# Recurrent block's output product: two interleaved groups of four column tiles in place of one group and four single products

## The chip, the cores and the metric

The kernel runs on one core of one Trainium2 chip. The metric is the device time of one execution in microseconds (us); lower is better. The engines are named as in the profile: PE is TensorE (matmuls), PEld its weight loads, DVE is VectorE, ACT is ScalarE, POOL is GpSimd, and SP is SyncE, which only issues DMAs.

## The reference, cut to what matters

The kernel is a trunk of two layers over x (512 positions of 1024 channels, float32). Layer 0 mixes positions with an RG-LRU recurrent block, layer 1 with an S5 block, and each is followed by a ConvFFN. The change is in the last line of the recurrent block, a product of y (512 x 1024) with a 1024 x 1024 matrix, and the sum with h behind it.

```python
def _rglru_mixer(h, w_in, conv_w, conv_b, w_a, b_a, w_x, b_x, lam, w_out):
    xg = h @ w_in
    xr, gate = xg[..., :D_RNN], xg[..., D_RNN:]
    xr = _causal_dwconv(xr, conv_w, conv_b)
...
    _, hs = lax.associative_scan(_real_scan_combine, (a, bterm), axis=1)
    y = hs.astype(h.dtype) * jax.nn.gelu(gate)
    return y @ w_out

...
    for i in range(DEPTH):
        hn = _rmsnorm(h, norm_mix_g[i])
...
        h = h + mix.astype(h.dtype)
        hn = _rmsnorm(h, norm_ffn_g[i])
        h = h + _conv_ffn(hn, ffn_w_up[i], ffn_conv_w[i], ffn_conv_b[i], ffn_w_down[i]).astype(h.dtype)
```

## The kernel before

**Layout.** All activations lie transposed, channels on the 128 partitions and the 512 positions along the free axis, as 8 tiles of 128 x 512 per 1024 channels. The residual h is 8 such tiles in SBUF. So a product's column tile m is one PSUM bank of 128 x 512, summed over 8 contraction tiles k.

**Precision.** Each operand is split into a high part and a low part of a 32-bit type that TensorE takes at full rate. mm3 (L215 to 218) issues three matmuls for each pair of k and m: high by high (L216), low of the activation by high of the weight (L217), high by low of the weight (L218). Weights come from DRAM as raw; ScalarE casts whi<-raw (L212) and VectorE makes wlo<-raw,whi (L200). An activation's pair is called ah and al, or nh and nl, by the pool it lies in.

**Jobs.** The program is a list of jobs, run by run(). A weighted job has one 512 KB piece of a weight, and 24 matmuls of 128 x 512. There are 200 of them, numbered here from 0; weights are loaded and split some jobs ahead. Jobs without a weight run between two weighted ones. Work on a job's result is put off with defer(ticks, phase, fn, cost): it is issued so many jobs later, in one of four phases of that job. Of the time of VectorE in a job that isn't spent so (5.1 us less the costs), a credit is kept, and from it the items of a background list bg are issued. The engines' queues take their instructions in the order that a scheduler of the language makes of all this, by its own estimate of when each is ready.

**Two shapes of product.** group() runs four jobs, each with two contraction tiles k for four column tiles, so it fills four banks at once, k outermost. product() is one job for one column tile, all eight k in one bank. Banks come from two pools of four: psA (tiles called pa) and psB (pb, and py, pv, pr, px, stat, rb, sps).

**The output product.** project() (L471) is a group() over column tiles 0 to 3 in psA (here A0 to A3), then a product() for each of tiles 4 to 7 in psB. It is jobs 16 to 23, and the FFN's first group follows as jobs 24 to 27. Its operand is y: out(c) (L615) multiplies scan and gate for chunk c and makes its high and low part (al<-g,ah), chunks 4 and 5 one job before 6 and 7. The step with contraction tiles 2s and 2s+1 reads chunks 2s and 2s+1. residual() (L339) defers the sum h<-h,pb by 1 or 2 jobs, and in the same job the next norm's parts: nl<-h, and acc<-acc,sq. Behind tile 7's it defers the norm's stat (TensorE), v and r (VectorE) and rb.

**mid.** Between the group and the first single product, project() runs the unweighted job mid: it closes the recurrent block's buffers and calls then(), which opens the FFN's buffers and starts s5_pre. This fills bg with the preparation of S5's tables: matrices by channel block that go to DRAM (d_K, d_P, d_T), with small matmuls into sps and copies se<-sps. Its last item, finish, defers the transfers d_T<-d_K on GpSimd's queue.

**S5.** s5() comes after the FFN (from job 92). S_(c) makes pv of a transposed input us by a transfer from DRAM (d); H_(c) makes hs from the scan of v (VectorE, tables co and si); TR(c) makes py from us and hs by turns, and ys<-py goes through DRAM (d<-ys, ge<-d) to E_(c), which makes ah and al of it. J[c] are the last four products of S5's input, A0[.] and B0[.], with brackets, the steps of the GLU product that reads E_'s results.

Of the kernel before, what the change touches and what calls it, by code (L numbers as in the profile page):

```python
# [19 lines left out]
P = 128  # L20
S = 512
D = 1024
KD = D // P
# [48 lines left out]
class Trunk:  # L72
# [395 lines left out]
        else:  # L468
            yield from down(NPART - 1)

    def project(self, w, x, next_gain, view=lambda h, ps: (h, ps), turn=0, mid=None):  # L471

        def post(pss):
            self.turn = turn
            self.next_gain = next_gain
            for m in range(4):
                self.residual(m, pss[m], view, d=1 + m // 2)
        yield from self.group(w, x, self.bankA, post)
        if mid:
            yield Job(None, mid)  # L480
        for m in range(4, KD):
            yield self.product(w, m, x, self.bankB, lambda ps, m=m: self.residual(m, ps, view))


    def rglru(self, x, g_first, late_tables, gt, w_in, w_a, w_x, w_out, next_gain, then):
# [127 lines left out]
        yh, yl = [], []  # L613
# [54 lines left out]
            st["ctx"].close()  # L668
            then()

        yield from self.project(w_out, lambda: (yh, yl), next_gain, mid=mid)


    def small(self, pool, n, name, dt=F32):
# [775 lines left out]
def lay_out(inp):  # L1450

    import numpy as np

    def columns(*vs):
        return np.concatenate([np.reshape(v, (-1, P)) for v in vs]).T

    def blocks(w, rows):

        return w.reshape(-1, P, w.shape[1])[:rows].transpose(1, 0, 2).reshape(P, -1)

    def wide(w, c0, n):

        return [blocks(w[r:r + n * P, c0:c0 + 1024 // n], n) for r in range(0, w.shape[0], n * P)]

    def tiles(w):
        return np.stack(wide(w, 0, 2) + [blocks(w[:, c:c + P], KD) for c in range(4 * P, w.shape[1], P)])

    def mixed(w, axis):

        s = list(w.shape)  # L1470
        v = w.reshape(s[:axis] + [KD, NGC, GC] + s[axis + 1:])
        return v.swapaxes(axis + 1, axis + 2).reshape(s)

    def halves(re, im):

        r, i = (v.transpose(2, 0, 1).reshape(v.shape[2], -1) for v in (re, im))
        return np.stack([np.concatenate([r, i]), np.concatenate([i, r])], 1)

    g = {k: np.asarray(v) for k, v in inp.items()}
    a = np.stack([g["s5_a_re"][0].T, g["s5_a_im"][0].T], 1)  # L1480
    t = lambda v: v[0].swapaxes(1, 2)
    return dict(
        x=g["x"][0].T,
        cols=columns(g["norm_mix_g"], g["norm_ffn_g"], g["norm_final_g"], g["rg_conv_w"][0], g["rg_conv_b"],
                     g["rg_b_a"], g["rg_b_x"], g["rg_lambda"], g["s5_d"]),
        ffn_cols=np.stack([columns(g["ffn_conv_w"][i], g["ffn_conv_b"][i]) for i in range(2)]),
        rg_w_in=tiles(g["rg_w_in"][0]),
        rg_w_a=g["rg_w_a"][0].swapaxes(0, 1),
        rg_w_x=g["rg_w_x"][0].swapaxes(0, 1),
        rg_w_out=tiles(g["rg_w_out"][0]),  # L1490
        s5_w_in=tiles(mixed(g["s5_w_in"][0], 1)),
        s5_a=np.concatenate([a, a]),
        s5_log_dt=g["s5_log_dt"],
        s5_b=halves(t(g["s5_b_re"]), t(g["s5_b_im"])),
        s5_c=halves(g["s5_c_re"][0], g["s5_c_im"][0]),
        s5_w_glu=np.stack([v for c in range(0, 2 * D, 4 * P) for v in wide(mixed(g["s5_w_glu"][0], 0), c, 2)]),
        s5_w_out=tiles(g["s5_w_out"][0]),
        ffn_w_up=np.stack([tiles(w) for w in g["ffn_w_up"]]),
        ffn_w_down=np.stack([[v for q in range(NPART) for n in [2 if i and q == NPART - 1 else FP]
                              for c in range(0, D, 1024 // n) for v in wide(w[q * FP * P:(q + 1) * FP * P], c, n)]  # L1500
                             for i, w in enumerate(g["ffn_w_down"])]),
        fin=np.reshape(g["norm_final_g"], (1, D)),
    )
# [20 lines left out]
```

## Time and profile before

| | |
|---|---|
| three timed runs | 1194.86, 1195.45, 1198.6 us |
| their median | 1195.45 us |
| the profiled execution | 1200.28 us |
| its span, first to last instruction | 1198.5 us |
| granted TensorE clock over the span | 0.995 |
| busy share PE, DVE, ACT | 99%, 74%, 44% |

The profile tells what each engine did in one execution. Busy time counts running instructions. A row of the timeline has a start, the time from start to end (matmuls overlap, so two starts tell the rate and the row's time doesn't), and in brackets the idle time before it with the instruction whose end ended it. The granted clock is the share of TensorE's full speed (2.4 GHz; the lower level is half).

### The profile page before, as it was taken

What the parts mean: (1) busy time and instruction counts of PE and PEld (TensorE: products, weight loads), DVE (VectorE), ACT (ScalarE), POOL (GpSimd) and SP (SyncE); (2) the same over time, 40 slices, a digit from 0 to 9 for tenths busy, and PEclk for the clock granted to TensorE, in tenths of its full rate; (3) what the DMA queues carried; (4) which work ended last, traced back from release to release, by engine and by line L of the source; (5) the groups of instructions that cost most, each with busy time, mean ns of one, the idle gap of its engine ahead of it and who ended that gap; (6) DMA issues with size and microseconds to landing.
All of it is one profiled execution on the core that took longest, in us unless ns stands there. A gap on an engine that the chain in (4) does not pass through costs nothing.

```text
span 1198.5 us, 14366 instructions
## 1 busy us (share of the span) xinstructions
PE 1180.9 (99%) x5456; PEld 974.9 (81%) x5456; DVE 884.1 (74%) x1463; ACT 524.6 (44%) x701; POOL 18.6 (2%) x35
## 2 busy tenths in 40 slices
PE   9999999999999999999998999999999999999997
PEld 7777888888778888888898888888888888888886
DVE  7899799998998998678587442658766757575755
ACT  5588425434334242446267242524433434242425
POOL 0000000000000000202001000000000000000000
PEclk9999999999999999999999999999999999999999
DMA  7212422247554444546576523222232323233321
GB/s 272 71 70 88 140 93 89 93 125 257 203 163 124 145 143 149 181 162 229 158 223 222 157 89 106 88 98 96 90 104 89 105 91 103 90 103 92 102 88 71
DMA packets 77558, 154.65 MB, mean 129 GB/s; under 512 B 26481, under 2 KB 40193, under 8 KB 77361
## 3 DMA queue, kind: packets, MB, share of 16 engines
q1 hardware_dynamic: 73376, 138.79, 35.9%
q0 software_dynamic: 4112, 14.94, 3.5%
q8 instruction: 43, 0.70, 0.2%
q14 instruction: 27, 0.21, 0.1%
HBM read 132.21 MB, written 23.86 MB: 130 GB/s over the span
## 4 chain that ended last, share of the span: by engine, by line
PE 69%; DMA 2%; DVE 1%; ACT 1%; issue 0%; SPq 0%; ACTq 0%
PE pa L218 13%; PE pa L217 13%; PE pa L216 12%; PE pb L216 9%; PE pb L217 9%; PE pb L218 9%; PE pv L1139 1%; DMA us<-d 1%; PE py L1181 1%; PE py L1180 1%; PE sps L1030 0%; DMA d<-up 0%; DMA ge<-d 0%; DMA d<-ys 0%; PE kps L1001 0%; PE ph L1327 0%
## 5 line engine op out<-in xcount | busy, mean ns | idle before, releaser
L212 ACT ACTIVATE whi<-raw 128x1024 fp32r<-128x1024 f32 (+1 forms) x201 | 211.7, 1053 | 390.9 <-PE pa L217 163.9
L200 DVE TENSOR_TENSOR wlo<-raw,whi 128x1024 fp32r<-128x1024 f32 (+1 forms) x201 | 245.0, 1219 | 101.3 <-ACT whi L212 89.5
L216 PE MATMUL pa<-nh,whi 128*128 128x512 f32 x520 | 208.1, 401 | 0.9 <-ACT whi L212 0.9
L218 PE MATMUL pa<-nh,wlo 128*128 128x512 f32 x520 | 203.3, 391 | 0.0
L217 PE MATMUL pa<-nl,whi 128*128 128x512 f32 x520 | 203.1, 391 | 0.0
L218 PE MATMUL pa<-ah,wlo 128*128 128x512 f32 x448 | 176.4, 394 | 0.0
L217 PE MATMUL pa<-al,whi 128*128 128x512 f32 x448 | 176.4, 394 | 0.0
L216 PE MATMUL pa<-ah,whi 128*128 128x512 f32 x448 | 173.4, 392 | 2.5 <-DVE g L200 1.4
L209 DVE SCALAR_TENSOR_TENSOR cv<-pad,t_f,cv 128x512 f32<-128x512 f32 x192 | 142.6, 750 | 1.8
L216 PE MATMUL pb<-ah,whi 128*128 128x512 f32 x320 | 125.5, 392 | 1.0 <-ACT se L212 1.0
L218 PE MATMUL pb<-ah,wlo 128*128 128x512 f32 x320 | 124.7, 390 | 0.0
L217 PE MATMUL pb<-al,whi 128*128 128x512 f32 x320 | 124.7, 390 | 0.0
L216 PEld LDWEIGHTS pa<-nh,whi 128*128 128x128 f32 x520 | 98.0, 189 | 24.4 <-issue 3.7
L217 PEld LDWEIGHTS pa<-nl,whi 128*128 128x128 f32 x520 | 98.2, 189 | 21.5 <-issue 1.7
L200 DVE TENSOR_TENSOR pad<-pa,rb 128x512 f32<-128x512 f32 x88 | 60.7, 690 | 74.1 <-PE pa L218 73.9
L218 PEld LDWEIGHTS pa<-nh,wlo 128*128 128x128 f32 x520 | 98.1, 189 | 20.8
L216 PE MATMUL pb<-nh,whi 128*128 128x512 f32 x280 | 110.0, 393 | 0.0
L217 PE MATMUL pb<-nl,whi 128*128 128x512 f32 x280 | 109.2, 390 | 0.0
L218 PE MATMUL pb<-nh,wlo 128*128 128x512 f32 x280 | 109.1, 390 | 0.0
L200 DVE TENSOR_TENSOR h<-h,pb 128x512 f32<-128x512 f32 x96 | 65.6, 686 | 55.8 <-PE pb L218 55.5
L216 PEld LDWEIGHTS pa<-ah,whi 128*128 128x128 f32 x448 | 84.3, 189 | 20.2 <-DVE g L200 1.8
L218 PEld LDWEIGHTS pa<-ah,wlo 128*128 128x128 f32 x448 | 85.0, 190 | 17.7
(285 smaller groups left out, 1478.6 us busy)
## 6 DMA issues: line engine op xcount, KB each, us to landing
raw<-in_ffn_w_up_dram SPq DMA_DIRECT2D x96, 512.0 KB, 3.5
raw<-in_ffn_w_down_dram SPq DMA_DIRECT2D x48, 512.0 KB, 3.5
raw<-in_s_w_glu_dram SPq DMA_DIRECT2D x16, 512.0 KB, 3.6
raw<-in_rg_w_in_dram SPq DMA_DIRECT2D x15, 512.0 KB, 3.6
mS<-d_P SPq DMA_DIRECT2D x8, 640.0 KB, 6.6
raw<-in_rg_w_out_dram SPq DMA_DIRECT2D x8, 512.0 KB, 3.5
d_T<-zero POOLq DMA_DIRECT2D x1, 4096.0 KB, 16.2
d_P<-se SPq DMA_DIRECT2D x16, 256.0 KB, 2.0
```

Source lines behind the costliest of these rows:

```text
L200: self.last_vec = self.nc.vector.tensor_tensor(out=out, in0=a, in1=b, op=op).ins
L209: self.nc.vector.scalar_tensor_tensor(out, a, s, b, op0, op1)
L212: self.nc.scalar.activation(out, a, func, **kw)
L216: mm(ps, wh, xh, start=start, stop=False)
L217: mm(ps, wh, xl, start=False, stop=False)
L218: mm(ps, wl, xh, start=False, stop=stop)
L1139: nc.tensor.matmul(pv[:, g * NCH:(g + 1) * NCH], mS[:, g * P:(g + 1) * P], us[:, g * NCH:(g + 1) * NCH], start=True, stop=True)
L1180: nc.tensor.matmul(o, mT[g // 4][:, gs], us[:, g * NCH:(g + 1) * NCH], start=True, stop=False)
L1181: nc.tensor.matmul(o, mR[g // 4][:, gs], hs[:, g, 0:NCH], start=False, stop=True)
```

## The change

A new project_late() takes the place of project() in the recurrent block; S5 keeps project(), which loses its parameter mid. The product is two groups, A (column tiles 0 to 3 in psA) and B (4 to 7 in psB), in the order A0 B0 A1 B1 A2 A3, then mid, then B2 B3. Each step has two contraction tiles, k outermost, but a group's last step has its column tiles outermost. The residual sums of a group are deferred from its last step, those of its first two tiles by one job and of the others by two. The weight is laid out to suit, still eight pieces of 512 KB.

mid is thus run before job 22 where it was before job 20; bg's last item, finish, is issued in job 84 where it was in job 80 (both counted by running the planner's arithmetic), and S5 starts at job 92 in both.

```diff
--- before.py
+++ after.py
@@ -468,7 +468,7 @@
         else:
             yield from down(NPART - 1)
 
-    def project(self, w, x, next_gain, view=lambda h, ps: (h, ps), turn=0, mid=None):
+    def project(self, w, x, next_gain, view=lambda h, ps: (h, ps), turn=0):
 
         def post(pss):
             self.turn = turn
@@ -476,10 +476,36 @@
             for m in range(4):
                 self.residual(m, pss[m], view, d=1 + m // 2)
         yield from self.group(w, x, self.bankA, post)
-        if mid:
-            yield Job(None, mid)
         for m in range(4, KD):
             yield self.product(w, m, x, self.bankB, lambda ps, m=m: self.residual(m, ps, view))
+
+    def project_late(self, w, x, next_gain, mid):
+
+
+        banks = [[], []]
+
+        def step(hf, s):
+            def emit(wh, wl):
+                if s == 0:
+                    banks[hf].extend((self.bankB if hf else self.bankA)() for _ in range(4))
+                xh, xl = x()
+                order = [(kk, m) for kk in range(2) for m in range(4)]
+                if s == 3:
+                    order = [(kk, m) for m in range(4) for kk in range(2)]
+                for kk, m in order:
+                    k = 2 * s + kk
+                    sl = slice(m * P, (m + 1) * P)
+                    self.mm3(banks[hf][m], wh[:, kk, sl], wl[:, kk, sl], xh[k], xl[k], k == 0, k == KD - 1)
+                if s == 3:
+                    self.next_gain = next_gain
+                    for m in range(4):
+                        self.residual(4 * hf + m, banks[hf][m], d=1 + m // 2)
+            return Job(w[4 * hf + s], emit, 2)
+
+        A, B = ([step(hf, s) for s in range(4)] for hf in range(2))
+        yield from [A[0], B[0], A[1], B[1], A[2], A[3]]
+        yield Job(None, mid)
+        yield from [B[2], B[3]]
 
 
     def rglru(self, x, g_first, late_tables, gt, w_in, w_a, w_x, w_out, next_gain, then):
@@ -668,7 +694,7 @@
             st["ctx"].close()
             then()
 
-        yield from self.project(w_out, lambda: (yh, yl), next_gain, mid=mid)
+        yield from self.project_late(w_out, lambda: (yh, yl), next_gain, mid)
 
 
     def small(self, pool, n, name, dt=F32):
@@ -1487,7 +1513,7 @@
         rg_w_in=tiles(g["rg_w_in"][0]),
         rg_w_a=g["rg_w_a"][0].swapaxes(0, 1),
         rg_w_x=g["rg_w_x"][0].swapaxes(0, 1),
-        rg_w_out=tiles(g["rg_w_out"][0]),
+        rg_w_out=np.stack(wide(g["rg_w_out"][0], 0, 2) + wide(g["rg_w_out"][0], 4 * P, 2)),
         s5_w_in=tiles(mixed(g["s5_w_in"][0], 1)),
         s5_a=np.concatenate([a, a]),
         s5_log_dt=g["s5_log_dt"],
```

How this moves instructions is shown at three places; tile numbers are the buffers of the build, and a line's number in the changed kernel is higher by up to 26.

PE, from the end of A0 to the second job of the output product. Before:

```order
L216 MATMUL pa_1036<-ah_928,whi_939 128x512
L217 MATMUL pa_1036<-al_929,whi_939 128x512
L218 MATMUL pa_1036<-ah_928,wlo_940 128x512
L216 MATMUL pa_1033<-ah_979,whi_987 128x512
L217 MATMUL pa_1033<-al_980,whi_987 128x512
L218 MATMUL pa_1033<-ah_979,wlo_988 128x512
L216 MATMUL pa_1034<-ah_979,whi_987 128x512
L217 MATMUL pa_1034<-al_980,whi_987 128x512
```

and now:

```order
L216 MATMUL pa_1036<-ah_928,whi_939 128x512
L217 MATMUL pa_1036<-al_929,whi_939 128x512
L218 MATMUL pa_1036<-ah_928,wlo_940 128x512
L216 MATMUL pb_1081<-ah_924,whi_987 128x512
L217 MATMUL pb_1081<-al_925,whi_987 128x512
L218 MATMUL pb_1081<-ah_924,wlo_988 128x512
L216 MATMUL pb_1082<-ah_924,whi_987 128x512
L217 MATMUL pb_1082<-al_925,whi_987 128x512
```

The second job was A1 (chunks 2 and 3 into the same banks pa); now it is B0, with A0's chunks 0 and 1 into four banks pb.

PE in S5 at the first step of TR(0), behind S_(2) (py is its bank, pb that of J[6]). Before:

```order
L217 MATMUL pb_5205<-nl_4920,whi_5049 128x512
L218 MATMUL pb_5205<-nh_4919,wlo_5050 128x512
L1139 MATMUL pv_5247<-us_5095,mS_4707 128x64 x8
L1180 MATMUL py_5268<-us_5083,ah_4691 128x64
L216 MATMUL pb_5303<-nh_4769,whi_5103 128x512
L217 MATMUL pb_5303<-nl_4770,whi_5103 128x512
L218 MATMUL pb_5303<-nh_4769,wlo_5104 128x512
L216 MATMUL pb_5303<-nh_4774,whi_5103 128x512
L217 MATMUL pb_5303<-nl_4775,whi_5103 128x512
L218 MATMUL pb_5303<-nh_4774,wlo_5104 128x512
L216 MATMUL pb_5303<-nh_4815,whi_5103 128x512
```

and now:

```order
L217 MATMUL pb_5205<-nl_4920,whi_5049 128x512
L218 MATMUL pb_5205<-nh_4919,wlo_5050 128x512
L1165 MATMUL pv_5247<-us_5095,mS_4707 128x64 x8
L1206 MATMUL py_5268<-us_5083,ah_4691 128x64
L1207 MATMUL py_5268<-hs_5178,al_4692 128x64
L1206 MATMUL py_5268<-us_5083,ah_4691 128x64
```

Matmuls of J[6] stood between TR(0)'s first product with us and its first with hs; now all of TR(0) stands together.

PE in S5 at S_(7) (pv_5696; pa is the bank group of A0, py_5640 that of TR(4), py_5717 of TR(5)). Before:

```order
L1181 MATMUL py_5640<-hs_5525,mR_5488 128x64
L1180 MATMUL py_5640<-us_5197,mT_5487 128x64
L1181 MATMUL py_5640<-hs_5525,mR_5488 128x64
L1139 MATMUL pv_5696<-us_5499,mS_5530 128x64
L217 MATMUL pa_5507<-al_5589,whi_5297 128x512
L218 MATMUL pa_5507<-ah_5588,wlo_5298 128x512
L217 MATMUL pa_5508<-al_5589,whi_5297 128x512
L218 MATMUL pa_5508<-ah_5588,wlo_5298 128x512
L217 MATMUL pa_5509<-al_5589,whi_5297 128x512
L218 MATMUL pa_5509<-ah_5588,wlo_5298 128x512
L217 MATMUL pa_5510<-al_5589,whi_5297 128x512
L218 MATMUL pa_5510<-ah_5588,wlo_5298 128x512
```

and now:

```order
L217 MATMUL pa_5508<-al_5668,whi_5395 128x512
L218 MATMUL pa_5508<-ah_5667,wlo_5396 128x512
L217 MATMUL pa_5509<-al_5668,whi_5395 128x512
L218 MATMUL pa_5509<-ah_5667,wlo_5396 128x512
L216 MATMUL pa_5510<-ah_5667,whi_5395 128x512
L217 MATMUL pa_5510<-al_5668,whi_5395 128x512
L218 MATMUL pa_5510<-ah_5667,wlo_5396 128x512
L1165 MATMUL pv_5696<-us_5499,mS_5530 128x64 x8
L1206 MATMUL py_5717<-us_5295,mT_5584 128x64
L1206 MATMUL py_5767<-us_5393,mT_5663 128x64
L216 MATMUL pa_5507<-ah_5744,whi_5395 128x512
L1207 MATMUL py_5717<-hs_5606,mR_5585 128x64
```

S_(7) was split, its first matmul ahead of the low parts of A0[1] (whi_5297) and the rest behind the first four of A0[2] (whi_5395); now it is whole and stands behind A0[2], directly ahead of TR(5).

## Rows read from the trace of the kernel before

**Rows 1.** The page's line of busy times.

```profile
PE 1180.9 (99%) x5456; PEld 974.9 (81%) x5456; DVE 884.1 (74%) x1463; ACT 524.6 (44%) x701; POOL 18.6 (2%) x35
```

**Rows 2.** All waits of PE: the instruction that waited, what it waited for, us in total, how often, the longest.

```profile
PE pv L1139 <- DMA us<-d: 2.2, 1, 2.2
PE py L1181 <- DVE hs L209: 1.5, 1, 1.5
PE pa L216 <- DVE g L200: 1.4, 1, 1.4
PE pa L216 <- ACT ah L212: 1.2, 1, 1.2
PE warm L502 <- DVE ones L98: 1.1, 1, 1.1
PE pb L216 <- ACT se L212: 1.0, 1, 1.0
PE pa L216 <- ACT whi L212: 0.9, 1, 0.9
```

**Rows 3.** Timelines of PE and of DVE at the first job of the output product (start, us, engine, line, operation, output and inputs, shape, count, idle before).

```profile
110.63 0.39 PE L216 MATMUL pa<-ah,whi 128*128 128x512 f32 x1
...
114.22 0.50 PE L216 MATMUL pa<-ah,whi 128*128 128x512 f32 x1 [1.38 <-DVE g L200]
...
111.25 2.34 DVE L593 TENSOR_TENSOR_SCAN ix<-q,ix 128x512 f32<-128x512 f32 x2
113.50 0.67 DVE L200 TENSOR_TENSOR g<-pa,rb 128x512 f32<-128x512 f32 x1
```

**Rows 4.** The same timelines further on: the low parts of chunks 4 and 5 and of 6 and 7 on DVE, and the first matmul of A2 and of A3 on PE.

```profile
120.99 1.29 DVE L200 TENSOR_TENSOR al<-g,ah 128x512 fp32r<-128x512 f32 x2
...
123.58 1.30 DVE L200 TENSOR_TENSOR al<-g,ah 128x512 fp32r<-128x512 f32 x2
...
123.21 0.39 PE L216 MATMUL pa<-ah,whi 128*128 128x512 f32 x1
...
128.65 0.39 PE L216 MATMUL pa<-ah,whi 128*128 128x512 f32 x1
```

**Rows 5.** Busy time of each engine in stretches of 6 us (the stretch, its length, busy time and instructions of PE, PEld, DVE, ACT, POOL, then granted clock, share of the DMA engines, GB/s): one in the group of four banks, two in the FFN behind the product.

```profile
124.00:130.00 6.00, 6.00 (x28) 4.96 (x27) 2.48 (x8) 2.16 (x3) 0.00 (x0) 1.00 0.43 124
...
160.00:166.00 6.00, 6.00 (x28) 4.99 (x27) 5.59 (x28) 1.06 (x1) 0.00 (x0) 1.00 0.27 98
166.00:172.00 6.00, 6.00 (x32) 5.05 (x32) 5.97 (x42) 1.06 (x1) 0.00 (x0) 1.00 0.31 104
```

**Rows 6.** Timelines of DVE and PE behind the product: the sum, the low part and the norm's sum of one column tile, the norm's stat, and the first matmul of the FFN's third step.

```profile
150.61 0.69 DVE L200 TENSOR_TENSOR h<-h,pb 128x512 f32<-128x512 f32 x1 [2.09 <-PE pb L218]
...
152.62 0.74 DVE L209 SCALAR_TENSOR_TENSOR nl<-h,t_gt,nh 128x512 fp32r<-128x512 f32 x1
153.28 0.68 DVE L200 TENSOR_TENSOR acc<-acc,sq 128x512 f32<-128x512 f32 x1
...
166.73 0.95 PE L297 MATMUL stat<-mean,acc 128*128 128x1 f32 x8
167.54 0.49 PE L216 MATMUL pa<-nh,whi 128*128 128x512 f32 x1
```

**Rows 7.** Timelines of DVE and PE: the low part of a weight, and the first matmul of the job that reads it.

```profile
181.80 1.25 DVE L200 TENSOR_TENSOR wlo<-raw,whi 128x1024 fp32r<-128x1024 f32 x1
...
190.37 0.39 PE L216 MATMUL pb<-nh,whi 128*128 128x512 f32 x1
```

**Rows 8.** Timelines of ACT and PE in the preparation of S5.

```profile
318.25 0.58 ACT L212 ACTIVATE se<-sps 128x512 f32<-128x512 f32 x1
...
318.88 0.50 PE L216 MATMUL pb<-ah,whi 128*128 128x512 f32 x1 [1.01 <-ACT se L212]
```

**Rows 9.** Timeline of POOL, which issues DMAs, and from the view of DMAs the last of the eight transfers (output and input, queue, count, size, us to landing).

```profile
489.11 6.06 POOL L1055 DMA_DIRECT2D d_T<-d_K  x8 [199.90 <-DMA d_K<-kk]
541.21 1.91 POOL L1118 DMA_DIRECT2D al<-d_P  x3 [46.04 <-PE pb L217]
...
d_T<-d_K POOLq DMA_DIRECT2D x1, 64.0 KB, 8.4
```

**Rows 10.** S5: timelines of PE and DVE at TR(0), the three waits of PE, the stretches of 10 us with their clock (columns as in rows 5), and from the view of DMAs the transfers us<-d.

```profile
604.75 0.39 PE L1180 MATMUL py<-us,ah 128*128 128x64 f32 x2
...
605.38 0.75 DVE L209 SCALAR_TENSOR_TENSOR hs<-vs,sgn,v 128x512 f32<-128x512 f32 x1
...
646.79 0.43 PE L1139 MATMUL pv<-us,mS 128*128 128x64 f32 x2 [2.15 <-DMA us<-d]
...
655.10 0.43 PE L1181 MATMUL py<-hs,mR 128*128 128x64 f32 x2 [1.52 <-DVE hs L209]
...
672.35 0.95 PE L216 MATMUL pa<-ah,whi 128*128 128x512 f32 x3 [1.16 <-ACT ah L212]
...
640.00:650.00 10.00, 7.84 (x52) 7.08 (x52) 6.66 (x12) 4.78 (x8) 1.06 (x2) 0.87 1.00 340
650.00:660.00 10.00, 8.48 (x51) 7.49 (x50) 7.32 (x13) 9.11 (x14) 0.00 (x0) 0.84 0.31 72
660.00:670.00 10.00, 10.00 (x63) 8.95 (x63) 6.33 (x11) 4.03 (x6) 1.07 (x2) 0.94 0.65 202
...
us<-d SPq DMA_DIRECT2D x8, 256.0 KB, 3.1
```

## The prediction

> **What bounds the kernel now.** I began with the busy times: TensorE is busy for 1180.9 of 1198.5 us, 99%, VectorE for 74% [rows 1]. So the time can only fall where TensorE waits, runs at the lower clock or does less, and the change leaves its work the same: 200 weighted jobs of 24 matmuls, those of the output product among them. Next I read the list of TensorE's waits, to see which of them the change can reach: seven, 9.3 us together [rows 2]. Then the timeline at the output product, to see where its wait sits: job A0 starts at 110.63 and stands still for 1.38 us before 114.22, for VectorE's g [rows 3]. A job without a wait takes 5.44 us (123.21 to 128.65 for A2 [rows 4]), 0.2267 us a matmul. Last I read S5's stretch, where three of the seven lie (those for us, hs and ah [rows 2]), and the granted clock there.
>
> The profiled execution took 1200.28 us, 1.8 more than its span and 4.8 more than the median of the three runs, 1195.45. Terms are summed against the profiled execution and then set against the median; as that run was the slowest seen, part of what it lost may be its own, and I discount for that.
>
> **The change, part by part.**
>
> *Matmuls.* Eight jobs of 24 before and after, on the same tile sizes: 0. The four products become the second group, so 96 matmuls now go round four banks where they filled one at a time. The first group does that already, at full clock and with TensorE busy throughout (6.00 of 6.00, 1.00 [rows 5]): 0.
>
> *The wait in A0.* The fourth bank of psA is freed by g<-pa,rb, which VectorE starts at 113.50 because a double scan of 2.34 us stands ahead [rows 3]. A0 is still the first step, takes the same four banks and stands behind the same scan: the 1.38 us stay. Gain 0.
>
> *The later y chunks.* A2, which needs y chunks 4 and 5, now runs two jobs later. Before, the lows of these were written by 122.28 (120.99 + 1.29) and A2 started at 123.21 with no wait; those of 6 and 7 by 124.88, A3 at 128.65 [rows 4]. A margin of 0.9 us becomes 0.9 + 10.9; there is no wait to take away. Direct gain 0 in this run; in a run where VectorE is a little later it would be some tenths.
>
> *The tail.* All eight residual adds now come after A3 and B3. B3 stands where the last of the four products did, which began just before the add at 150.61; with its tiles outermost its first one is done six matmuls later, at about 152. What needs the adds: FFN's third step at 167.54, the first to read rows 4 and 5, and the norm's stat at 166.73 [rows 6]. The upper four rows cost an add of 0.69, a low of 0.74 and a sum of 0.68 each, 8.4 us of VectorE; with one wlo of 1.25 between [rows 7] the last would be done at about 161.7, 5 us before stat. Queued behind an add that waits on VectorE would be the next wlo, with the margin of the next part. So 0; without that margin a wait like the 1.38 of rows 3.
>
> *The background.* mid moves from before the fifth job of the product to before the seventh (from job 20 to 22). The S5 preparation, with its tables, starts two jobs later, and falls together with the adds. The planner's credit, by its own costs, gets 3.4 us lower than before at the worst (-5.64 for -2.24), so VectorE runs up to 3.4 us late there, in windows in which it is already busy for 5.59 and 5.97 of 6 us [rows 5]. Behind it on VectorE stand the lows of the next weights. The least margin of these is at the one written at 181.80 to 183.05 and read at 190.37 [rows 7]: 7.3 us, more than 3.4. Covered: 0; without cover a job would wait for the missing part. Later in the preparation its sps matmuls share a bank with a pb tile, and TensorE waits 1.01 us, until 318.88, for ScalarE's se, which starts at 318.25 [rows 8]. Now two matmuls of another bank come between, 0.45 us: 0.5 us gained; from 0 to 1.0.
>
> *Queues.* The eight transfers d_T<-d_K go out on GpSimd's queue at 489.11 and land up to 8.4 us later; the queue's next entries start at 541.21 [rows 9]. Four jobs later, where this step now falls, is 22 us: landed by 519. Still hidden: 0.
>
> *S5's order.* Its text is untouched, but the scheduler places its instructions by when it thinks them ready, and that has shifted; this is the only place where TensorE's row moves outside the product and the preparation by more than a few places. In this run S5 lost 2.15 at 646.79 (S_(7) waits for its input's transfer), 1.52 at 655.10 (TR(5) waits for hs) and 1.16 at 672.35, 4.8 us together, and the granted clock fell to 0.87, 0.84 and 0.94 of full in three windows of 10 us, 3.5 us of work lost [rows 10]. So 8.3 us were lost. The low stretches follow the waits of 2.15 and 1.52, while none follows those of 1.38, 1.16 and 1.01 [rows 2].
> (a) TR(0): the seven matmuls of J[6] between its first us and its first hs matmul are gone. hs is written at 605.38 + 0.75 = 606.13; the us matmul starts at 604.75 and the hs one would 0.2 later [rows 10]: 1.2 us lost, which is under the smallest wait that dropped the clock.
> (b) S_(7) starts behind the lows of A0[1] and the whole of A0[2], 8 + 12 = 20 matmuls or 4.5 us later, and its input was 2.15 us late: that wait goes, and its low clock (half of 3.5: 1.7) with it: 3.9 us gained.
> (c) TR(5) and A0[3] then stand right behind S_(7) and need hs(5) and E_(3)'s ah, which now gate by themselves. Nearest rows are the waits of 1.52 and 1.16 there: from 0.3 (if VectorE and ScalarE, idle while S_(7) waited, also come 2.15 earlier) to 3.1, and if one idle is long a low stretch of 1.7 again. I take 2.0 and half a low stretch, 0.9.
> (d) J[7] takes a bank that ScalarE's ys(0) frees close to when it is wanted: 0 to 0.5; I take 0.2.
> After: 1.2 + 2.0 + 0.9 + 0.2 = 4.3 lost, bounds 1.5 (1.2 + 0.3) and 6.5 (1.2 + 3.1 + 1.7 + 0.5). Gain 8.3 - 4.3 = 4.0, bounds 1.8 and 6.8.
>
> *Sum.* 0.5 + 4.0 = 4.5 us against the profiled run. The median run is 4.8 us below that, and since the losses of S5 depend on transfers, I expect the timed runs to lose less there than the profiled one: I take two thirds, 3 us. 1195.45 - 3 = 1192.5.
>
> **Rivals.**
>
> *A wash.* The wait that interleaving could take away, one for a y chunk, isn't in the trace, and S5's order moves the same losses to other instructions: 1.2 at TR(0), and at S_(7)'s successors the same transfer. For it: ScalarE and VectorE are the ones behind, not TensorE; against it: VectorE was idle while S_(7) waited. 1194 to 1197.5.
>
> *Full repayment.* (c) at its lower end and no low clock: 6.8 + 0.5 to 1.0, so 1188, from 1186 to 1190.5. For it: both low stretches follow waits that the order could remove; against it: TR(0)'s new one.
>
> *Slower: a chain in S5.* TR(0) late makes ys(0) late by 1.2 us, and it is followed in order on ScalarE by the casts for the next S_ steps, so d, ge and E_(c) come late in turn; with TR and A0 steps contiguous nothing lies between to fill in. Each idle of 1.5 us or more then costs a low stretch (1.7 us) too: 3.2 us a time. Three such idles (9.6 us) would be about what is lost now; it decides from the fourth on: four or five, with TR(0)'s 1.2 under the bound left out, lose 12.8 to 16.0, which is 4.5 to 7.7 more than 8.3: 1199 to 1204. For it: S_ and TR steps stand as 24 matmuls in a row, and the round trip over DRAM behind each is two transfers, 3.1 us for one of them [rows 10]; against it: each job of filler between two of these is still there.
>
> *Slower: the clock in the product.* The rows show a group that goes round four banks at 1.00 of full clock [rows 5]. If going round eight of them let TensorE idle briefly between tiles and its clock fell, 192 matmuls at the lower of the two levels, 1.2 for 2.4 GHz, would take twice 0.2267 us each and add 43.5 us: 1239. The Trainium skill (TensorE: Matmul & The Clock Gate, section "A second HAM failure mode: psum-queue depth-cycling") tells of a kernel that cycled through PSUM banks in which "the PE micro-idles between MM groups frequently enough that HAM oscillates"; by that rule, this is what the change would bring. The trace disagrees for four banks, by the 1.00 above.
>
> **How the numbers follow.** A measurement of this kernel can tell about 0.3% from no change: 3.6 us, so faster is below 1191.9 and slower above 1199.0. The forecast (S5 partly repaid, the rest nothing) gets 0.52, 1189.5 to 1195, its middle just inside the bound: 0.22 faster, 0.30 same. A wash 0.16, same. Full repayment 0.17, faster. The chain in S5 0.13 and the clock in the product 0.02 are slower. So 0.39 faster, 0.46 same, 0.15 slower. The range leaves out half of the full repayment's lower part and most of the slower cases: 1187.0 to 1199.5.
>
> **What would show it.** In the changed kernel's profile: the product's two groups at 0.2267 us a matmul and clock 1.00; the wait of 1.4 us in A0 still there, and no other before FFN; the wait for se at about half of 1.01; in the list of waits no us<-d of 2 us, a new one of about 1.2 at TR(0) for hs, and one or two behind S_(7); granted clock in S5 low in one stretch at most. I am wrong if the wait in A0 is gone, if stat, rb or an FFN step waits, if a wlo gates a job between 155 and 200 us, or if S5's waits with its low clock sum to more than 8.3 us.

## The result and the profile after

The changed kernel took 1203.2 us in the median of six runs (1200.61 to 1204.22), the kernel before 1195.31 in six (1194.78 to 1199.02; three of them are those of the table ahead of the prediction). The two medians are 7.9 us apart; the ratio on record, which is no quotient of these two, is 1.0051, 95% interval 1.0040 to 1.0061. By the ratio the changed kernel is slower by about 6 us, outside the range and on the other side of the forecast.

The profiled execution of the changed kernel took 1200.61 us, the fastest of its six; that of the kernel before, 1200.28, was slower than all six of its. So the two traces end 0.3 us apart and don't show the difference as a sum; the single waits do. TensorE's waits in the changed kernel (columns as in rows 2):

```profile
PE py L1206 <- DMA mT<-d_T: 2.4, 1, 2.4
PE pa L216 <- DVE g L200: 1.4, 1, 1.4
PE warm L528 <- DVE ones L98: 1.1, 1, 1.1
PE py L1207 <- DVE hs L209: 1.0, 1, 1.0
PE pa L216 <- ACT whi L212: 0.9, 1, 0.9
PE pa L218 <- DVE wlo L200: 0.5, 1, 0.5
```

Against [rows 2]: the wait for g in A0 stayed; those for us, se and ah are gone; hs gates another step; the one for mT wasn't foreseen. Timelines of PE, DVE and POOL behind the product and in the preparation:

```profile
113.60 0.50 PE L216 MATMUL pa<-ah,whi 128*128 128x512 f32 x1 [1.38 <-DVE g L200]
...
160.30 0.69 DVE L200 TENSOR_TENSOR acc<-acc,sq 128x512 f32<-128x512 f32 x1
...
504.50 6.06 POOL L1081 DMA_DIRECT2D d_T<-d_K  x8 [188.57 <-DMA d_K<-kk]
539.55 1.91 POOL L1144 DMA_DIRECT2D al<-d_P  x3 [29.00 <-PE pb L217]
```

These answer to [rows 3, 6, 9]: the same 1.38; the last residual part at 160.99, 0.7 us ahead of the estimate; the d_T transfers 15.4 us later and still 35 us ahead of what is queued behind them. To see in which stage time is lost, take the norm's stat, the last matmuls of the recurrent block, of its FFN and of S5. In the kernel before and then in the changed one:

```profile
166.73 0.95 PE L297 MATMUL stat<-mean,acc 128*128 128x1 f32 x8
...
575.65 0.95 PE L297 MATMUL stat<-mean,acc 128*128 128x1 f32 x8
...
803.74 0.94 PE L297 MATMUL stat<-mean,acc 128*128 128x1 f32 x8
```

```profile
166.10 0.95 PE L297 MATMUL stat<-mean,acc 128*128 128x1 f32 x8
...
574.00 0.95 PE L297 MATMUL stat<-mean,acc 128*128 128x1 f32 x8
...
803.90 0.95 PE L297 MATMUL stat<-mean,acc 128*128 128x1 f32 x8
```

The second stretch, FFN and preparation, is 407.90 for 408.92: 1.0 us gained. The third, S5, is 229.90 for 228.09, although the one of before is from an execution 5 us above its median. In S5 the granted clock is low from 600 to 620 us, where the kernel before has 1.00, and lower than in [rows 10] from 660 to 670; from 640 to 660, where [rows 10] have 0.87 and 0.84, it is 1.00 (columns as there):

```profile
600.00:610.00 10.00, 8.96 (x57) 8.55 (x56) 9.83 (x17) 7.98 (x13) 0.00 (x0) 0.81 0.65 223
610.00:620.00 10.00, 10.00 (x53) 8.57 (x53) 9.32 (x15) 6.04 (x11) 0.00 (x0) 0.84 0.42 130
...
660.00:670.00 10.00, 7.61 (x38) 7.03 (x37) 5.38 (x8) 3.50 (x6) 0.00 (x0) 0.72 0.64 211
670.00:680.00 10.00, 10.00 (x58) 8.73 (x57) 0.78 (x5) 2.07 (x4) 0.00 (x0) 0.94 0.25 79
```

The first two windows lose 0.35 x 10 = 3.5 us of work and the last two 3.4. PE and DVE at TR(0), where the first stretch begins, and PE at its end:

```profile
603.23 0.39 PE L1206 MATMUL py<-us,ah 128*128 128x64 f32 x2
604.66 0.43 PE L1207 MATMUL py<-hs,al 128*128 128x64 f32 x2 [1.04 <-DVE hs L209]
...
606.04 0.39 PE L1207 MATMUL py<-hs,al 128*128 128x64 f32 x2
606.27 0.60 PE L1206 MATMUL py<-us,ah 128*128 128x64 f32 x2
606.66 0.64 PE L1207 MATMUL py<-hs,al 128*128 128x64 f32 x2
...
612.75 0.57 PE L217 MATMUL pb<-nl,whi 128*128 128x512 f32 x1
613.16 0.39 PE L218 MATMUL pb<-nh,wlo 128*128 128x512 f32 x1
...
603.86 0.74 DVE L209 SCALAR_TENSOR_TENSOR hs<-vs,sgn,v 128x512 f32<-128x512 f32 x1
```

TensorE idles for 1.04 us until hs is written at 604.60. From 606.27 its rows are half as fast, until 613.16: 6.9 us, 3.4 lost. The second place is TR(7), whose first matmul stands ahead of TR(6); POOL issues its matrix mT only when TR(5) has ended and its buffer is free:

```profile
657.74 0.28 PE L1207 MATMUL py<-hs,mR 128*128 128x64 f32 x1
...
663.00 0.41 PE L1206 MATMUL py<-us,mT 128*128 128x64 f32 x2 [2.39 <-DMA mT<-d_T]
...
658.09 0.54 POOL L1146 DMA_DIRECT2D mT<-d_T  x1 [7.52 <-PE py L1207]
```

So 1.04 + 3.5 + 2.39 + 3.4 = 10.3 us are lost there, where the prediction put 4.3. That is 2.0 more than the 8.3 of the kernel before's trace, and the third stretch is 1.8 longer.

### The profile page after: what moved, and what is told of

It is laid out like the page before. It is cut to its first block, busy times and chain, and to the rows that moved or that the text cites. A ratio compares the mean times of both kernels' runs of the same rounds, so it can differ in the third digit from the quotient of the medians.

```text
span 1198.7 us, 14360 instructions
## 1 busy us (share of the span) xinstructions
PE 1182.8 (99%) x5456; PEld 976.4 (81%) x5456; DVE 885.1 (74%) x1463; ACT 524.1 (44%) x701; POOL 18.6 (2%) x35
## 4 chain that ended last, share of the span: by engine, by line
PE 92%; DVE 4%; ACT 2%; DMA 1%; issue 1%; SPq 0%; ACTq 0%; DVEq 0%
PE pa L216 17%; PE pa L218 17%; PE pa L217 17%; PE pb L216 12%; PE pb L217 12%; PE pb L218 12%; PE py L1207 1%; PE py L1206 1%; PE pv L1165 1%; DVE wlo L200 1%; DMA raw<-in_rg_w_in_dram 1%; PE sps L1056 1%; DVE xc L209 0%; DVE q L209 0%; ACT thr L212 0%
```

## The experiments

Theory 1: S5's order costs the time, and nothing else of the change does. Theory 2: the interleaved product and its late residual sums do. Theory 3: the preparation, two jobs later. Theory 4: mid's place acts on S5 otherwise than by the order. Each ratio is to runs of the kernel before on the same chip, with its 95% interval. In these rounds the kernel before took 1197.8 to 1198.4 us in the median of 15 to 35 runs, more than the 1195.31 above, so ratios are compared and not times.

**e1, e2: the two parts of the change apart.** e1 keeps the new product and puts mid back; e2 keeps the old product and moves mid:

```diff
--- changed, e1
-        yield from [A[0], B[0], A[1], B[1], A[2], A[3]]
+        yield from [A[0], B[0], A[1], B[1]]
         yield Job(None, mid)
-        yield from [B[2], B[3]]
+        yield from [A[2], A[3], B[2], B[3]]
--- before, e2
-        if mid:
-            yield Job(None, mid)
         for m in range(4, KD):
+            if mid and m == 6:
+                yield Job(None, mid)
             yield self.product(w, m, x, self.bankB, lambda ps, m=m: self.residual(m, ps, view))
```

> The changed kernel, with the unweighted job mid back before the fifth job of the product (A0 B0 A1 B1, mid, A2 A3 B2 B3). TensorE's row in S5 is then the row of the kernel before, step by step. Theory 1 (S5's new row costs the time, and mid's place alone brings that row): 1195.3 within 2 us, a ratio of 0.998 to 1.002. Theory 2 (the interleaved product and its late residual sums cost the time, by VectorE's backlog or FFN's first steps): stays at 1201 to 1204.

> The kernel before, with its old product, and only mid moved two jobs later (before the seventh job). TensorE's row in S5 is then that of the changed kernel but for two matmuls of S_(7). Theory 1: 1201 to 1204, a ratio near 1.005, and the waits of S5 in the profile are those of the changed kernel (hs at TR(0), mT at TR(7)). Theory 2: 1195.3 within 2 us. Theory 3 (the preparation, two jobs later, costs the time between 150 and 580 us): 1201 to 1204 as well, but then with S5 not starting earlier than in the kernel before, and no more waiting in S5.

e1: 0.9991 (0.9978 to 1.0005). e2: 1.0041 (1.0027 to 1.0055). e1 has the order of the kernel before in S5 on every queue, e2 that of the changed one but for a few places on TensorE and more of them on VectorE. Theory 2 falls: the product costs nothing that can be told from zero, and mid's place alone brings the loss (the interval of e2's 1.0041 overlaps that of 1.0051). Theory 3 falls by e2's trace: stat to stat the preparation takes 407.44 us (165.55 to 572.99), less than before, and S5 231.70 (to 804.69). e2's windows at TR(0) and its wait there:

```profile
600.00:610.00 10.00, 8.95 (x55) 8.44 (x55) 9.93 (x16) 7.99 (x13) 0.00 (x0) 0.79 0.48 173
610.00:620.00 10.00, 10.00 (x58) 8.72 (x57) 9.87 (x16) 6.67 (x12) 0.00 (x0) 0.87 0.64 175
```

```profile
PE py L1181 <- DVE hs L209: 1.0, 1, 1.0
```

**e3 to e6: TensorE's row tied by code written in another order.** S5's steps are split (TR(c, lo, hi) and S_(c, lo, hi) issue part of their matmuls), hk issues a part inside another job behind its n-th matmul, and each matmul of S5 is tied behind the one before it. e3, an excerpt:

```diff
-        yield from [H_(1), S_(2), TR(0)]
-        yield J[6]
+        yield from [H_(1), S_(2), TR(0, 0, 1)]
+        yield hk(J[6], {7: [TR(0, 1, 16)]})
...
-        yield A0[0]
-        yield from [H_(4), S_(5), TR(3), E_(1), A0[1]]
-        yield from [H_(5), S_(6), TR(4), E_(2)]
-        yield A0[2]
+        yield hk(A0[0], {4: [H_(4), S_(5), TR(3, 0, 11)]})
+        yield from [TR(3, 11, 16), E_(1)]
+        yield hk(A0[1], {4: [H_(5), S_(6), TR(4), E_(2), H_(6), S_(7, 0, 1)]})
+        yield hk(A0[2], {4: [S_(7, 1, 8), TR(5, 0, 1), TR(6, 0, 1), TR(5, 1, 11)]})
```

e4 writes the changed kernel's row into the kernel before in the same way, e5 has only the first of these edits, and e6 writes TR(7) as one piece behind A0[4].

> The changed kernel (interleaved product, mid before job 22), with TensorE's instructions in S5 tied one behind the other in exactly the row that the kernel before has. Theory 1 (TensorE's row in S5 is the cost): the ratio falls from 1.005 to between 0.997 and 1.001, and TR(0) waits for nothing. Theory 4 (what follows mid's place on the other engines and queues is the cost: VectorE, ScalarE or transfers later in S5): stays at 1.003 to 1.006.

> The kernel before (old product, mid before job 20), with TensorE's instructions in S5 tied in the row of the changed kernel (but for one matmul of B0[0]). Theory 1: a ratio of 1.004 to 1.007, with a wait for hs of about 1 us in TR(0) and low clock behind it. Theory 4: 0.998 to 1.002.

> The changed kernel with its own row in S5, but the seven matmuls of J[6] back between the first and the second instruction of TR(0). If the wait of 1.0 us there and the low clock behind it (3.4 us) are one cost of the change: 4.4 us less than the changed kernel, a ratio of 1.000 to 1.003. If the clock falls anyway in the dense row of S_ and TR steps: 1 us less, a ratio of 1.003 to 1.005.

> The changed kernel with its own row in S5, but the first instruction of TR(7) no longer ahead of TR(6): it stands behind A0[4]. If the wait for mT (2.4 us) and its low clock (3.4 us) are due to that place: up to 5.8 us less, a ratio of 0.999 to 1.003, the smaller the gain the more of it TR(6) and A0[4] lose by waiting themselves for hs, ah or mR. If not: 1.004 to 1.006.

e3: 1.0079 (1.0051 to 1.0106). e4: 1.0116 (1.0093 to 1.0139). e5: 1.0058 (1.0041 to 1.0074). e6: 1.0032 (1.0021 to 1.0043). e3, e4 and e5 lie above both of the ranges given for them: e3, with TensorE's row of the kernel before, is slower than the changed kernel. Its longest wait and e5's say why (e4's is another, 5.5 us for VectorE's al):

```profile
PE pb L219 <- ACT ys L212: 2.6, 1, 2.6
```

```profile
PE pb L219 <- ACT ys L212: 2.7, 1, 2.7
```

J[7] waits for the bank that ScalarE's ys(0) frees, a wait that neither kernel has. Code written in another order gave ScalarE, VectorE and SyncE other rows too: in e3 twelve copies of tables and of v (si, co, vs, rho) stand ahead of ys(0) that stood behind it. ScalarE's ys(0) in e3 and in the kernel before:

```profile
620.94 0.60 ACT L212 ACTIVATE ys<-py 128x512 f32<-128x512 f32 x1
```

```profile
610.11 0.60 ACT L212 ACTIVATE ys<-py 128x512 f32<-128x512 f32 x1 [2.05 <-PE py L1181]
```

So "TensorE's row" was too narrow, and e3 to e5 can't tell theory 1 from 4. e6 left the other queues as in the changed kernel but for a few places, and falls between its two ranges. TR(7) no longer waits there, but another wait for mT has come, of TR(6)'s first matmul for its own matrix, with 3.4 us of low clock behind it; so e6 doesn't tell what TR(7)'s place costs:

```profile
656.18 0.41 PE L219 MATMUL py<-us,mT 128*128 128x64 f32 x2 [1.32 <-DMA mT<-d_T]
```

**e7, e8: the order of all five queues.** The code stays as it is, and at its end each S5 instruction is tied behind the one that comes before it on its queue in the other kernel's build (ROWS holds the 1057 of them by queue):

```diff
+def tie_rows(tc):
+    by = {i.name: i for i in tc.nc.cur_bb.bb.instructions}
+    how = mybir.DependencyInfo(mybir.DependencyClass.NoSync, mybir.DependencyReason.DATA)
+    for row in ROWS.values():
+        names = [f"I-{a + b * i}" for a, b, n in row for i in range(n)]
+        for x, y in zip(names, names[1:]):
+            tc.add_manual_dep(by[y], x, how, reason="row")
...
     K.run(jobs())
+    tie_rows(tc)
```

> The changed kernel with the order of the kernel before on all five queues in S5 (TensorE, VectorE, ScalarE, GpSimd, SyncE: 1057 instructions, each tied behind the one before it on its queue); the product and mid's place stay as changed. Theory 1, now for all queues and not for TensorE's row alone: the whole loss is gone, a ratio of 0.997 to 1.001. Theory 4 (mid's place acts on S5 otherwise than by the order, by transfers or buffers that come later): 1.003 to 1.006.

> The kernel before with the order of the changed kernel on all five queues in S5; its product and mid's place stay. Theory 1: the changed kernel's loss without its product, a ratio of 1.004 to 1.008, with TensorE's waits for hs at TR(0) and for mT at TR(7). Theory 4: 0.998 to 1.002.

e7: 0.9992 (0.9982 to 1.0001). e8: 1.0043 (1.0029 to 1.0056). Both as theory 1 had them, and theory 4 falls: the order carries the loss from one kernel to the other, whole as far as the intervals tell, and the changed kernel without it is level with the kernel before. That the ties cost nothing by themselves is seen in e1, which has e7's order in S5 without ties and 0.9991. e8 shows both waits, for mT at TR(7) and for hs at TR(0):

```profile
PE py L1180 <- DMA mT<-d_T: 1.9, 1, 1.9
PE py L1181 <- DVE hs L209: 1.0, 1, 1.0
```

**e9, e10, e13: which places of the order.** Now single edits on TensorE's row, all other queues tied as they were. In e9 the changed kernel has J[6]'s seven matmuls back inside TR(0); in e10 the kernel before has them taken out; e13 is e9 with TR(7)'s first matmul back behind A0[4]. TR0, J6 and the like stand for the numbers of these matmuls in the row of PE:

```diff
--- changed, e9 and e13
-    TR0[0:16], J6[0:24],
+    TR0[0:1], J6[0:7], TR0[1:16], J6[7:24],
--- changed, e13
-    A0_3[1:12], TR7[0:1], B0_0[0:1], TR6[1:16], A0_4, TR7[1:16], A0_5, B0_0[1:12],
+    A0_3[1:12], TR6[1:16], A0_4, TR7[0:16], A0_5, B0_0[0:12],
--- before, e10
-    TR0[0:1], J6[0:7], TR0[1:16], J6[7:24],
+    TR0[0:16], J6[0:24],
```

> The changed kernel with its own order on all queues in S5 but for one edit on TensorE's: the seven matmuls of J[6] stand between the first instruction of TR(0) and its others again. If the wait at TR(0) and the low clock behind it are paid once: 4.4 us less than the changed kernel, a ratio of 1.000 to 1.003. If the wait comes back at J[7], whose bank ys(0) frees: 1.003 to 1.006.

> The mirror of it: the kernel before with its own order on all queues in S5, but TR(0) in one piece with the 24 matmuls of J[6] behind it. If a wait of 1.0 us inside S_(2) and TR(0) costs its 1.0 and 3.4 of low clock: a ratio of 1.003 to 1.005. If it costs the 1.0 alone, or shortens the later waits by as much: 0.999 to 1.002.

> The changed kernel with its own order on all queues in S5 but for two edits on TensorE's: the seven matmuls of J[6] back inside TR(0), as in e9, and TR(7)'s first instruction behind A0[4] rather than ahead of TR(6) (with the one matmul of B0[0] that followed it). If the places of these two steps are the whole loss: a ratio of 0.998 to 1.001. If more of the order costs: as e9, 1.001 to 1.003.

e9: 1.0017 (1.0001 to 1.0034). e10: 1.0033 (1.0020 to 1.0046). e13: 0.9982 (0.9968 to 0.9997). TR(0)'s place costs 0.33% or 4.0 us in the kernel before (2.4 to 5.5), and taking it back gives the changed kernel 0.34% of its 0.51 (by the two intervals 0.14 to 0.54). Taking TR(7)'s place back too gives another 0.35% (0.13 to 0.57), the rest and perhaps more. e10's windows and e9's:

```profile
600.00:610.00 10.00, 8.95 (x54) 8.42 (x53) 9.83 (x17) 6.40 (x10) 0.00 (x0) 0.81 0.70 246
610.00:620.00 10.00, 10.00 (x40) 8.32 (x39) 4.58 (x8) 3.39 (x5) 0.00 (x0) 0.68 0.54 158
```

```profile
600.00:610.00 10.00, 10.00 (x70) 9.15 (x69) 9.94 (x16) 7.52 (x12) 0.00 (x0) 1.00 0.57 200
610.00:620.00 10.00, 9.24 (x65) 8.44 (x64) 8.65 (x14) 6.47 (x11) 0.00 (x0) 1.00 0.40 132
```

e10 loses 5.1 us to the clock behind a wait of 1.05; in e9 the clock stays full there, and a wait of 0.8 has moved to J[7]. How TR(7)'s place costs its part these two traces don't show: neither has a wait for mT. Both have waits for al and ah on either side of S_(7) (1.48 and 0.79 in e9, 1.02 and 0.89 in e13) and lose 5.1 us to the clock behind them, so TensorE comes to TR(7) later.

**e11, e12, e14: the wait filled, not shortened.** Matmuls whose result the next one overwrites are put into the bank that is about to be used, all queues tied: five ahead of TR(0) in the changed kernel (e11); seven ahead of S_(7) and six ahead of TR(5) in e7 (e12) and in the kernel before (e14).

```diff
                 py = self.bankB("py")
+                for _ in range(FILL_TR.get(c, 0)):
+                    nc.tensor.matmul(py, self.hh[0][:, 0:P], self.hh[1], start=True, stop=True)
...
                 us, mS = b["us"], b["S"]
+                for _ in range(FILL_S.get(c, 0)):
+                    nc.tensor.matmul(pv, self.hh[0][:, 0:P], self.hh[1], start=True, stop=True)
```

> The changed kernel with its own order on all queues in S5 and five matmuls more (128x512, their result is overwritten, 1.13 us) ahead of TR(0)'s first, in its own bank, so that TensorE works while hs is made. The wait isn't shortened, only filled. If the clock falls because TensorE idles there, the 3.4 to 5.1 us of low clock go and the wait's 1.0 stays: a ratio of 1.000 to 1.002. If it falls because of the dense row of small matmuls: as the changed kernel, 1.004 to 1.006.

> The changed kernel with the order of the kernel before on all queues in S5 (as e7), and matmuls of the same kind ahead of the two steps that wait there: seven ahead of S_(7), six ahead of TR(5). If the low clock behind these waits is due to the idle: 1.7 to 5 us less than e7, a ratio of 0.995 to 0.998. If the fill only moves the waits, or costs where there is none: 0.999 to 1.002.

> The kernel before with its own order on all queues in S5 and the same matmuls of fill as e12, seven ahead of S_(7) and six ahead of TR(5). It tells what of e12's gain is the fill and what the changed product and mid's later place. If the fill: 0.997 to 0.999, as e12. If the product: 0.999 to 1.001.

e11: 1.0019 (1.0007 to 1.0032). e12: 0.9981 (0.9972 to 0.9991), faster than both kernels. e14: 0.9988 (0.9978 to 0.9999). e11's windows at TR(0), and e12's where [rows 10] have 0.84 and 0.94:

```profile
600.00:610.00 10.00, 10.00 (x70) 9.17 (x69) 9.83 (x17) 7.37 (x12) 0.00 (x0) 1.00 0.69 239
610.00:620.00 10.00, 10.00 (x70) 9.20 (x69) 9.83 (x16) 6.00 (x11) 0.00 (x0) 1.00 0.36 106
```

```profile
650.00:660.00 10.00, 9.38 (x70) 8.64 (x68) 9.73 (x18) 6.86 (x12) 1.08 (x2) 1.00 0.45 102
660.00:670.00 10.00, 8.45 (x48) 7.05 (x48) 4.73 (x6) 3.55 (x5) 0.00 (x0) 1.00 0.64 215
```

In e11 hs comes no earlier after S_(2), the row of small matmuls is as dense as in the changed kernel, and the clock stays full at TR(0): the idle dropped it, not the dense row. The ratio falls by 0.32% or 3.8 us (0.16 to 0.48%), so most of TR(0)'s cost is clock, not wait. e11's profiled execution, at 1202.31 one of its slowest (median 1200.63), loses 8.5 us to the clock further on, behind a wait of 1.81 for al at 649.48. e12 is 0.11% below e7, where 1.7 us or more were expected; the intervals don't part the two, nor e14 from e12. What the fill shows plainly is the clock: over the span it is 0.996 to 0.999 in all 23 runs of e12 and e14, and 0.993 to 0.997 in the runs of the kernel before beside them. e12's twelve runs lie within 1.2 us (1195.18 to 1196.39), e14's eleven within 2.8, e7's twelve, at a clock of 0.993 to 0.997, within 5.1.

## Why the prediction was wrong

**The step that failed** is (a) under S5's order: TR(0)'s wait "under the smallest wait that dropped the clock". The wait was sized well, 1.04 us for 1.2. The low clock was priced at nothing, from three waits in [rows 2] that had none behind them, and it was 3.5 us there, 5.1 in e10. With it the term is 4.5 for 1.2, and e10 and e9 measure 4.0 and 4.1. The three rows were no bound: ahead of those of 1.38, 1.16 and 1.01 stand a dozen or more 128x512 matmuls, with at most four smaller ones behind these, while this one is in a row of 128x64 ones. The 1.52 of [rows 10], in such a row, was the nearer. The sign that the prediction gave for being wrong, more than 8.3 us of waits and low clock in S5, is there: 10.3.

**(c)** held a wait behind S_(7) of 0.3 to 3.1 for hs(5) or ah, with half a low stretch; it doesn't say how these ends come from its two rows, 1.52 and 1.16. There was one of 2.39 for another reason, mT: TR(7)'s first matmul ahead of TR(6), its buffer free only after TR(5). The build showed the place, and mT's row of transfers wasn't read against it. With 3.4 of low clock it is 5.8 for 2.9 in this trace. In the timed runs e13 against e9 puts TR(7)'s place at 0.35%, 4.2 us; by which wait is not shown, as neither trace waits for mT.

With both places taken back (e13) the changed kernel has 0.9982 (0.9968 to 0.9997) of the time before, and the forecast of 1192.5 was 0.9975: these two places are about what the forecast lacked.

**(b)** held in the trace, the wait for us went; but it was less of a gain than 3.9, since the timed runs of the kernel before lost less than its profiled one. The discount to two thirds was for this, and too small: e1 with the same order lost a single wait of 1.8 us in S5 and 3.4 to the clock behind it, and ran in 1196.40. In e14 the waits at S_(7) and TR(5) are filled and no low clock is left in S5, and the kernel before gains 0.12% by it, 1.4 us (0.1 to 2.6).

**What held.** The product: no cost, no gain (e1, e7). A window of 6 us in it (columns as in rows 5):

```profile
142.00:148.00 6.00, 6.00 (x29) 4.95 (x28) 5.92 (x9) 5.42 (x9) 0.00 (x0) 1.00 0.29 90
```

This is the end of A3 and B2, banks pa and then pb. TensorE is busy throughout at full clock, and windows of 6 us from 116 to 158, with the turns of A0 B0 A1 B1 among them, read the same 6.00 and 1.00. The rule of the Trainium skill (TensorE: Matmul & The Clock Gate, section "A second HAM failure mode: psum-queue depth-cycling") would have had it idle and slow there; the trace disagrees. The wait for g stays, 1.38. The tail, the weights' lows between 155 and 200 us and the d_T queue cost nothing. The wait for se went, 1.0 us for the 0.5 given. (d) didn't appear in the changed kernel; it does in e9, 0.8, where TensorE, at full clock, comes to J[7] at 617.1 and ScalarE ends ys(0) at 617.8.

**The rival "a chain in S5"** gave 1199 to 1204, where the time came to lie, but by four or five idles of 1.5 us or more each. It took two, of 1.04 and 2.39. Its first link, that TR(0) late makes ys(0) late, isn't what the trace shows: TR(0) ends at 609.9 and ys(0) starts at 617.90, behind nine copies of tables and of v that ScalarE's new order puts ahead of it.

**Open.** Whether the product with mid's later place is worth its 1.0 us: the traces show it between the stats, but 0.9992 for e7 and 0.9981 for e12 against e14's 0.9988 don't part it from nothing. By which wait TR(7)'s place costs the timed runs of e9 their 0.35% isn't shown. Why mid's place changes the scheduler's order in S5 was not traced.

## What to carry to other kernels

Where a scheduler sets the order, an edit far from a tight stage can cost more there than where it is made: compare the order of every queue in the tight stages, not only TensorE's. To find out whether an order is the cause, tie all queues to the other kernel's order and leave the code alone; code written in another order moves the other queues too. Price a wait among small matmuls with a stretch of half clock behind it, and where it can't be removed, fill it with matmuls whose result is overwritten; here that brought 0.1 to 0.3%.

## What the runs showed of the hardware

An idle of 1.04 us at TR(0), in a row of 128x64 matmuls, was followed by 6.9 us at the lower of the two clock levels, while 1.38 us between 128x512 matmuls was followed by none in the same trace. Nor was a longer one in e12, behind twelve 128x512 matmuls and two of 128x64, with 1.00 in the windows from 650 to 680:

```profile
667.65 0.99 PE L218 MATMUL pa<-ah,whi 128*128 128x512 f32 x3 [1.55 <-ACT ah L214]
```

All six traces in which the wait at TR(0) stands and TR(0) is in one piece (changed, e2, e4, e6, e8, e10) have a low stretch behind it; the one with the wait filled (e11) has not. The loss there is 3.4 us in four of them and 5.1 in e8 and e10. It isn't paid in every execution: e8's runs have a clock over the span of 0.990 (1206.62 us) to 0.997 (1198.36 us), and 0.998 is what the traces of e12 and e14 have with no low stretch in S5. So the run at 0.997 lost about 1 us to the clock in S5, by an estimate from these figures, less than the 5.1 at TR(0) in e8's trace.
